# Small TensorE products of a hybrid encoder layer padded to the whole array, or their parts stacked in the rows of one float32r product

## Chip, core and metric

The kernel runs on one core of one Trainium2 chip. The metric is the device time of one execution in microseconds (us), taken as the median of several runs. Engines are named TensorE (PE in rows, its weight loads PEld), VectorE (DVE), ScalarE (ACT), GpSimd (POOL) and SyncE (SP).

## What is computed

One layer of an encoder on 512 tokens of width 2048, ahead of which 16 learned meta tokens stand (L = 528). Three branches read column groups of one projection and are projected back together:

```python
h = concatenate([meta, x], axis=1)
u = rmsnorm(h, norm_w)
proj = u @ w_in
(gq, gk, gv, ggate, gcode, dq, dk, dv, dgate, z, xbc, dt_raw) = jnp.split(proj, split_idx, axis=-1)
glog = log_sigmoid(einsum('blzr,zrk->blzk', gcode, gla_wa2) + gla_ba) / GLA_TAU
o_gla = rmsnorm(bidirectional(gla_chunk_scan, ...), gla_norm_w) * silu(ggate)
o_diff = diff_attention(dq, dk, dv, lam, lambda_init, rel_bias, diff_norm_w) * silu(dgate)
y = bidirectional(ssd_chunk_scan, (xs, dt, a, Bm, Cm), ...)
o_ssd = rmsnorm((y + xs * ssd_D) * silu(z), ssd_norm_w)
h = h + concatenate([o_gla, o_diff, o_ssd], axis=-1) @ w_out
out = rmsnorm(h, final_norm_w)[:, N_META:]
```

Everything is float32. The meta tokens are the reason for most products with few rows: 528 positions are four blocks of 128 and one of 16.

## The kernel before, in words

The two large projections run in float32r, with each operand split into a high and a low part and three products summed (`uh`, `ul` for the normalised tokens, `whi`, `wlo` for the weights, `mm3` for the smaller products of this kind). Weights stream in as `wraw`; ScalarE rounds them to `whi` (L72) and VectorE subtracts to `wlo` (L132). All products go through the helper `mm` at L39, so their rows in the profile have one line and are told apart by tiles: results into `pm` buffers are the large projections, results into `pb` buffers the small products. Each pool has four buffers of PSUM.

The program is written as generators of tiles in plain order: load and normalise, transpose the tokens (`features`, L265), project the decay and B/C columns, SSD group 0 and 1 (`ssd_group`), then gated linear attention in head pairs (`decays`, `tok`), the relative-bias table, differential attention (`attention`, `softmax`, `values`), output projection, final norm. The order on each engine is not that of the text: a scheduler simulates the program and lays each engine's queue by it. Each engine then works its queue strictly in order, and waits on semaphores for operands and free buffers.

The products with few contraction rows, all in plain float32 (two instructions each in the profile; the transposes are one):

- L265, 16 meta-token rows of `mt` transposed against a 16 x 16 identity, 16 times, one for each 128 columns of width
- L322 and L324, the 64 rows of `comb` (decay and gate codes) transposed, five times
- L513 in `state`, `Btm` (16 rows x 128) by `xe` (16 x 512), the meta tokens' contribution to the SSD state, once in each of the two groups, after the loop over the four chunks of the group
- L585 in `decays`, `wa` (32 rows: the low-rank gate weights of both directions) by `comb`, two halves of 264 positions for each of four heads: eight products
- L651, `Em` (64 rows x 16) transposed, once for each head
- L671, `km` (16 rows x 64) by `vm`, once for each head
- L747, `rb` (32 buckets x 4 heads) by a one-hot matrix of 512, 512 and 16 columns, which makes the relative-bias table
- L830 in `values`, `wT2` by `vm`, both 16 rows, the meta tokens' share of attention's output, once for each of four heads and four query blocks

```python
v, vm = vd[h]
nc.tensor.transpose(po[0:NM, 128:256], w_[:, 512:528], ident)
wT2 = small.tile([NM, P], F32, name="wT2", bufs=2)
nc.vector.tensor_copy(wT2, po[0:NM, 128:256])
for c in range(4):
    mm(nc, po[:, 0:P], wT[:, c * P:(c + 1) * P], v[:, c], c == 0, False)
mm(nc, po[:, 0:P], wT2, vm, False, True)
```

The table goes through DRAM: written as `tabd`, copied four times to `tabr` (L754), and read as one tile `bt` for each head (L773), all on the DMA queue that GpSimd issues. `bt` has one buffer, so the tile of the next head is issued when the last addition of the head before has read it. The gate weights `wa` are loaded by that queue too, at the start of the kernel (L568 to L570).

Of the kernel before, what the change touches and what calls it, by code (L numbers as in the profile page):

```python
# [42 lines left out]
def encoder_kernel(ctx, tc, x, meta, rel_bias, final_norm_w, norm_w, w_in, w_out, gla_wa2, gla_ba,  # L43
# [46 lines left out]
    nc.scalar.activation(warm, warm, AF.Exp)  # L90
    for i in range(2):
# [167 lines left out]
    def features(parts, us):  # L259
        for k in range(KT):  # L260
            pt = pb()
            n = 0
            for t in parts:
                rows = NM if t == 4 else P
                nc.tensor.transpose(pt[:, n:n + rows], xt[t, k // 4][0:rows, (k % 4) * P:(k % 4 + 1) * P],  # L265
                                    ident[0:rows, 0:rows])
                n += rows
            cpy(uh[k][:, us], pt[:, 0:n], scale=nw[:, k:k + 1])
            stt(ul[k][:, us], pt[:, 0:n], nw[:, k:k + 1], uh[k][:, us].bitcast(F32), ALU.mult, ALU.subtract)
# [178 lines left out]
    def ssd_group(g, em):  # L448
# [17 lines left out]
        Btm = small.tile([NM, P], F32, name="Btm", bufs=2)  # L466
# [25 lines left out]
        for c in range(NC):  # L492
            py = pb()
            for i, m in enumerate(em):
                if c == 0:
                    tt(m, m, sc, ALU.mult)  # L496
                for hh in (slice(0, 64), slice(64, P)):
                    mm(nc, py[hh, i * 64:(i + 1) * 64], m[:, c, hh], xk[c][:, i * 64:(i + 1) * 64])
            ys = slot("o" if g else "ya", [P, 512], name="ya")
            yacc[g, c] = ys  # L500
            gtt(h3(ys), h3(xk[c]), hb(dfac[:, c, G8]), ALU.mult)
            tt(ys, py, ys, ALU.add)
# [32 lines left out]
        Sf = state(0, 4, None)  # L535
        Sb = state(1, 3, None)
# [11 lines left out]
    def tok(acc, tag, cuts, name):  # L548
# [11 lines left out]
        vm = small.tile([NM, P], F32, name=name + "m", bufs=4 if name == "vd" else 2)  # L560
        nc.vector.tensor_copy(vm, pt[0:NM, 0:P])
# [16 lines left out]
    def decays(h, reset):  # L578
# [36 lines left out]
        Em = small.tile([64, NM], F32, name="Em", tag="Em")  # L615
# [12 lines left out]
    def gla_pair(p, dd):  # L628
# [7 lines left out]
        for i in range(2):  # L636
# [25 lines left out]
        for i in range(2):  # L662
# [3 lines left out]
            v, vm = tok(t1([(C_GV + h * P, P, 0)]), "ya", (NM, 0), "gv")  # L666
# [99 lines left out]
    vd = [tok(t1([(C_DV + h * P, P, 0)]), "ya", (0, 512), "vd") for h in range(4)]  # L766
# [50 lines left out]
    def values(h, b, w_, rr):  # L817
# [8 lines left out]
        wT2 = small.tile([NM, P], F32, name="wT2", bufs=2)  # L826
        nc.vector.tensor_copy(wT2, po[0:NM, 128:256])
# [117 lines left out]
def _consts():  # L945
# [14 lines left out]
    onehot = (np.arange(32)[:, None] == bucket[None, :]).astype(np.float32)  # L960
    pick = np.zeros((P, 2, 16), np.float32)
# [25 lines left out]
```

## Time and profile before

| what | value |
|---|---|
| runs, median (lowest to highest, n) | 935.36 us (935.08 to 935.91, 3) |
| the profiled execution | 932.87 us |
| its span, first to last instruction | 931.1 us |
| mean granted TensorE clock | 0.991 |
| TensorE busy | 896.7 us (96%), 5750 products |
| VectorE, ScalarE, GpSimd busy | 552.0, 377.1, 177.5 us |
| TensorE's longest wait | 12.2 us for the vectors' load at the start |
| DMA | 88.06 MB, 96 GB/s of HBM over the span |

In the rows below, times are in microseconds unless marked ns. `16*128` ahead of the shapes of a product is its contraction rows times its output partitions, so `128*32` is a product over all rows with 32 outputs. `x2` is the number of instructions that a row stands for; a timeline row gives the start of the first and the time until the end of the last. Matmuls are pipelined, so one starts before the other ends: the distance of two starts is what a product costs in a full queue, and the busy time of one is longer. In square brackets stands the idle time ahead of an instruction and what ended it.

### The profile page before, as it was taken

What the parts mean: (1) busy time and instruction counts of PE and PEld (TensorE: products, weight loads), DVE (VectorE), ACT (ScalarE), POOL (GpSimd) and SP (SyncE); (2) the same over time, 40 slices, a digit from 0 to 9 for tenths busy, and PEclk for the clock granted to TensorE, in tenths of its full rate; (3) what the DMA queues carried; (4) which work ended last, traced back from release to release, by engine and by line L of the source; (5) the groups of instructions that cost most, each with busy time, mean ns of one, the idle gap of its engine ahead of it and who ended that gap; (6) DMA issues with size and microseconds to landing.
All of it is one profiled execution on the core that took longest, in us unless ns stands there. A gap on an engine that the chain in (4) does not pass through costs nothing.

```text
span 931.1 us, 14454 instructions
## 1 busy us (share of the span) xinstructions
PE 896.7 (96%) x5750; PEld 787.2 (85%) x5750; DVE 552.0 (59%) x1043; ACT 377.1 (40%) x734; POOL 177.5 (19%) x212
## 2 busy tenths in 40 slices
PE   4998999999999999999999999999999999999996
PEld 3898998997778788999999999888888888888884
DVE  6569976989957686853642466665552633232334
ACT  6555524336434386734222345554332432121322
POOL 1006203449334412010040000000120001020200
PEclk9999999999999999999999999999999999999998
DMA  8322232321133234123236332324223442223224
GB/s 243 97 69 62 75 83 56 85 74 46 47 90 87 74 92 110 48 67 91 75 75 190 90 83 72 94 80 134 80 80 90 151 144 91 92 95 107 91 91 181
DMA packets 99523, 88.06 MB, mean 95 GB/s; under 512 B 8223, under 2 KB 75415, under 8 KB 99455
## 3 DMA queue, kind: packets, MB, share of 16 engines
q1 hardware_dynamic: 95183, 77.06, 29.2%
q0 software_dynamic: 1392, 4.84, 1.8%
q10 hardware_dynamic: 2880, 5.24, 1.7%
q8 instruction: 45, 0.74, 0.3%
q14 instruction: 23, 0.19, 0.1%
HBM read 82.91 MB, written 6.34 MB: 96 GB/s over the span
## 4 chain that ended last, share of the span: by engine, by line
PE 84%; DVE 8%; issue 2%; DMA 2%; ACT 2%; SPq 1%; POOL 0%; ACTq 0%; POOLq 0%; DVEq 0%
PE pm L39 71%; PE pb L39 9%; DVE acc L394 2%; DMA xt<-in_x_dram 1%; DVE wlo L132 1%; PE pb L867 1%; PE pb L821 1%; PE pb L265 1%; DMA gn<-in_diff_norm_w_dram 1%; SPq L86 1%; DVE sg L431 1%; SPq L214 0%; DVE m L496 0%; ACT whi L72 0%; DVE acc L392 0%
## 5 line engine op out<-in xcount | busy, mean ns | idle before, releaser
L132 DVE TENSOR_TENSOR wlo<-wraw,whi 128x1024 fp32r<-128x1024 f32 (+1 forms) x128 | 167.3, 1307 | 205.0 <-ACT whi L72 204.5
L72 ACT ACTIVATE whi<-wraw 128x1024 fp32r<-128x1024 f32 (+1 forms) x134 | 137.2, 1025 | 301.5 <-PE pm L39 228.6
L39 PE MATMUL pm<-ul,whi 128*128 128x272 f32 (+2 forms) x960 | 226.7, 301 | 0.0
L39 PE MATMUL pm<-uh,whi 128*128 128x272 f32 (+2 forms) x960 | 222.5, 299 | 0.0
L39 PE MATMUL pm<-uh,wlo 128*128 128x272 f32 (+2 forms) x928 | 217.1, 299 | 0.1
L39 PEld LDWEIGHTS pm<-ul,whi 128*128 128x128 f32 x960 | 156.7, 190 | 7.9 <-issue 3.0
L39 PEld LDWEIGHTS pm<-uh,whi 128*128 128x128 f32 x960 | 156.2, 191 | 5.8 <-ACT uh L72 0.3
L39 PEld LDWEIGHTS pm<-uh,wlo 128*128 128x128 f32 x928 | 150.7, 190 | 6.0 <-issue 0.7
L39 PE MATMUL pm<-wlo,uh 128*128 128x512 f32 x256 | 102.3, 400 | 0.2 <-DVE wlo L132 0.2
L39 PE MATMUL pm<-whi,ul 128*128 128x512 f32 x256 | 101.2, 396 | 0.0
L39 PE MATMUL pm<-wlo,mh 128*128 128x512 f32 x256 | 100.7, 395 | 0.0
L39 PE MATMUL pm<-whi,ml 128*128 128x512 f32 x256 | 100.4, 394 | 0.0
L39 PE MATMUL pm<-whi,uh 128*128 128x512 f32 x256 | 95.5, 398 | 0.0
L39 PE MATMUL pm<-whi,mh 128*128 128x512 f32 x256 | 90.3, 394 | 0.0
L115 POOL TENSOR_TENSOR rs_r<-rs_v,mhalf 128x1 f32<-128x1 f32 (+1 forms) x28 | 20.0, 715 | 275.8 <-DVE rs_v L114 203.8
L39 PEld LDWEIGHTS pm<-whi,ul 128*128 128x128 f32 x256 | 48.4, 189 | 11.5 <-issue 1.1
L39 PEld LDWEIGHTS pm<-wlo,uh 128*128 128x128 f32 x256 | 48.4, 189 | 11.4 <-DVE wlo L132 0.7
L39 PEld LDWEIGHTS pm<-whi,ml 128*128 128x128 f32 x256 | 48.2, 188 | 11.3
L39 PEld LDWEIGHTS pm<-whi,mh 128*128 128x128 f32 x256 | 48.1, 188 | 11.1
L39 PEld LDWEIGHTS pm<-whi,uh 128*128 128x128 f32 x256 | 48.3, 189 | 10.8
L39 PEld LDWEIGHTS pm<-wlo,mh 128*128 128x128 f32 x256 | 48.1, 188 | 10.9
L901 POOL TENSOR_TENSOR hx<-hx,fw 128x512 f32<-128x512 f32 x12 | 18.1, 1542 | 164.9 <-ACT junk L888 164.9
(291 smaller groups left out, 1186.3 us busy)
## 6 DMA issues: line engine op xcount, KB each, us to landing
wraw<-in_w_in_dram SPq DMA_DIRECT2D x96, 512.0 KB, 3.7
wraw<-in_w_out_dram SPq DMA_DIRECT2D x30, 512.0 KB, 3.6
xt<-in_x_dram SPq DMA_DIRECT2D x16, 256.0 KB, 5.7
hx<-in_x_dram ACTq DMA_DIRECT2D x16, 256.0 KB, 3.7
out_dram<-hx SPq DMA_DIRECT2D x16, 256.0 KB, 2.9
tabr<-tabd POOLq DMA_DIRECT2D x4, 520.0 KB, 9.0
bt<-tabr POOLq DMA_DIRECT2D x4, 456.0 KB, 3.7
fw<-in_final_norm_w_dram ACTq DMA_DIRECT2D x4, 256.0 KB, 4.5
```

The source lines that it names most:

```text
L39: nc.tensor.matmul(out, lhsT=lhsT, rhs=rhs, start=start, stop=stop)
L72: nc.scalar.activation(out, in_, AF.Copy, **kw)
L86: nc.sync.dma_start(xt[t, j], xv[t][:, j * 512:(j + 1) * 512])
L115: gtt(r[0:rows, 0:cols], v[0:rows, 0:cols], mhalf[0:rows, 0:cols], ALU.pow)
L132: tt(lo, raw, hi.bitcast(F32), ALU.subtract)
L265: nc.tensor.transpose(pt[:, n:n + rows], xt[t, k // 4][0:rows, (k % 4) * P:(k % 4 + 1) * P], ident[0:rows, 0:rows])
L394: stt(acc, xp[:, k:k + L], cw[:, k:k + 1], acc, ALU.mult, ALU.add)
L431: stt(sg[:, c], px[:, c * P:(c + 1) * P], Xs[:, 1, c, h:h + 1], sg[:, c], ALU.subtract, ALU.min)
L821: nc.tensor.transpose(pt[:, c * P:(c + 1) * P], w_[:, c * P:(c + 1) * P], ident)
L867: nc.tensor.transpose(pt[:, c * P:(c + 1) * P], src[:, j * P:(j + 1) * P], ident)
L901: gtt(hx[t, b], hx[t, b], fw[b], ALU.mult)
```

## The change

A tile `zp` of zeros (128 x 15 x 64) is cut into slots that hold the 16-row operands `vm` (four slots `vz`), `wT2` (two, `wz`), `km` (two, `kz`) and the 64-row `Em` (four, `ez`). Copies write only the filled rows, and the products run over all 128 rows. The meta-token tile `mt` and the lower half of `comb` are cleared by GpSimd, and their transposes use the whole identity. Three products get their high and low parts stacked in the contraction rows of one float32r product of 96 rows: `BE` and `XE` for the SSD meta tokens (high, high, low by high, low, high at rows 0, 32 and 64), `WA` and `CS` for the gates, `RB` and a one-hot matrix of 96 rows for the bias table. The meta tokens' SSD state `Sf = state(0, 4, None)` is written ahead of the chunk loop, which moves the definitions of `state` and `yoff` up, unchanged apart from the branch for `c == 4`. `wa` is no longer a constant of its own but takes a slot of the shared work pool. The scratch for software-issued DMA is set to 8192.

```diff
+    zp = const.tile([P, 15, 64], F32, name="zp")
+    nc.vector.memset(zp, 0.0)
+    vz = [zp[:, 2 * i:2 * i + 2].rearrange("p a b -> p (a b)") for i in range(4)]
...
+    XE = const.tile([96, 512], F32R, name="XE")
+    BE = const.tile([96, P], F32R, name="BE")
+    RB = const.tile([96, 4], F32R, name="RB")
+    cpy(XE, zp[0:96, 0:8].rearrange("p a b -> p (a b)"))
...
         mt = wpool.tile([P, 1024], F32, name="mt", tag="whi" if i else "wlo")
+        nc.gpsimd.memset(mt, 0.0)
...
-                nc.tensor.transpose(pt[:, n:n + rows], xt[t, k // 4][0:rows, (k % 4) * P:(k % 4 + 1) * P],
-                                    ident[0:rows, 0:rows])
+                nc.tensor.transpose(pt[:, n:n + P], xt[t, k // 4][:, (k % 4) * P:(k % 4 + 1) * P], ident)
...
     comb = const.tile([P, L], F32, name="comb")
+    nc.gpsimd.memset(comb[64:P], 0.0)
...
+    CS = const.tile([96, L], F32R, name="CS")
+    cpy(CS[0:32], comb[0:32])
+    cpy(CS[64:96], comb[0:32])
+    tt(CS[32:64], comb[0:32], CS[0:32].bitcast(F32), ALU.subtract)
...
-        nc.vector.tensor_copy(Btm, pt[0:NM, 0:P])
+        cpy(BE[0:NM], pt[0:NM, 0:P])
+        cpy(BE[32:32 + NM], pt[0:NM, 0:P])
+        tt(BE[64:64 + NM], pt[0:NM, 0:P], BE[0:NM].bitcast(F32), ALU.subtract)
...
             if c == 4:
-                mm(nc, p_, Btm, xe[0:rows])
+                cpy(XE[0:NM], xe[0:NM])
+                cpy(XE[64:64 + NM], xe[0:NM])
+                tt(XE[32:32 + NM], xe[0:NM], XE[0:NM].bitcast(F32), ALU.subtract)
+                mm(nc, p_, BE, XE)
...
-    wa = const.tile([32, 4, P], F32, name="wa")
+    WA = const.tile([96, 4, P], F32R, name="WA")
+    wa = slot("w", [32, 4, P], name="wa")
     nc.gpsimd.memset(wa, 0.0)
...
+    cpy(WA[0:32], wa)
+    cpy(WA[32:64], wa)
+    tt(WA[64:96], wa, WA[0:32].bitcast(F32), ALU.subtract)
...
-            mm(nc, pg[:, 0:HL], wa[:, h, :], comb[0:32, hs])
+            mm(nc, pg[:, 0:HL], WA[:, h, :], CS[:, hs])
...
-            nc.tensor.transpose(pt[0:NM, 0:64], Em, ident[0:64, 0:64])
-            km = small.tile([NM, 64], F32, name="km", bufs=2)
-            nc.vector.tensor_copy(km, pt[0:NM, 0:64])
+            nc.tensor.transpose(pt[0:NM, 0:P], ez[2 * p + i], ident)
+            km = kz[i]
+            nc.vector.tensor_copy(km[0:NM], pt[0:NM, 0:64])
...
+        ohr = slot("w", [96, 512], F32R, name="ohr")
+        cpy(ohr[:, 0:n], oh[:, 0:n])
-        mm(nc, p_[0:4, 0:n], rb, oh[:, 0:n])
+        mm(nc, p_[0:4, 0:n], RB, ohr[:, 0:n])
...
-        wT2 = small.tile([NM, P], F32, name="wT2", bufs=2)
-        nc.vector.tensor_copy(wT2, po[0:NM, 128:256])
+        wT2 = wz[b % 2]
+        nc.vector.tensor_copy(wT2[0:NM], po[0:NM, 128:256])
...
-    nc = bacc.Bacc("TRN2", target_bir_lowering=False, num_devices=1)
+    nc = bacc.Bacc("TRN2", target_bir_lowering=False, num_devices=1, dynamic_dma_scratch_size=8192)
```

Two places show how the scheduler lays the queues now. The first is TensorE at the SSD meta-token product of group 0, before:

```order
L39 MATMUL pm<-uh_120,wlo 128x272
L39 MATMUL pm<-uh_120,wlo 128x256
L39 MATMUL pm<-uh_121,whi 128x272
L39 MATMUL pm<-uh_121,whi 128x256
L487 MATMUL pb<-masks,acc 128x128 x4
L39 MATMUL pb<-xk,m 64x64 x64
L39 MATMUL pb<-xe,Btm 128x512
L39 MATMUL pm<-ul_137,whi 128x272
```

and in the changed kernel:

```order
L39 MATMUL pm<-uh_121,whi 128x272
L39 MATMUL pm<-uh_121,whi 128x256
L39 MATMUL pm<-ul_137,whi 128x272
L39 MATMUL pm<-ul_137,whi 128x256
L39 MATMUL pb<-XE,BE 128x512
L39 MATMUL pb<-xk,m 64x64 x64
L39 MATMUL pb<-xs,Bt 128x512 x3
L39 MATMUL pm<-uh_121,wlo 128x272
```

The product has moved from behind the 64 small products of the chunk loop (`xk,m`) to ahead of them, and the first product of the next state (`xs,Bt`) now stands right behind the 64, where before a column of the large projection stood.

The second is TensorE at the first gate products, before:

```order
L39 MATMUL pm<-whi,uh_122 128x512
L39 MATMUL pb<-Ss,CTs 128x512
L39 MATMUL pb<-comb,wa 128x264
L39 MATMUL pb<-Ss,CTs 128x512 x2
L39 MATMUL pb<-comb,wa 128x264 x2
L39 MATMUL pm<-wlo,uh_122 128x512
L39 MATMUL pm<-whi,ul_138 128x512
```

and in the changed kernel, where `CS,WA` are the stacked operands:

```order
L39 MATMUL pm<-wlo,uh_134 128x512
L39 MATMUL pm<-whi,ul_150 128x512
L39 MATMUL pm<-whi,uh_135 128x512
L39 MATMUL pm<-wlo,uh_135 128x512
L39 MATMUL pm<-whi,ul_151 128x512
L39 MATMUL pb<-CS,WA 128x264 x4
L39 MATMUL pm<-wlo,uh_134 128x512
L39 MATMUL pm<-whi,ul_150 128x512
```

Before, one and then two products stand between the last SSD output products (`Ss,CTs`); now four stand together, later, among the products of the next projection. What they wait for has moved too, on GpSimd, which issues the load of the gate weights. Before, at the start:

```order
L108 MEMSET mhalf 128x8
L241 MEMSET ssq 128x1 x5
L568 MEMSET wa 32x512
L608 MEMSET zr 64x4
L740 DMA rb<-in_rel_bias_dram 32x4
L882 MEMSET hss 128x4
L570 DMA wa<-in_gla_wa_dram 16x4x64 x2
```

and in the changed kernel, behind the SSD additions (`ya` is the running SSD output, `Sn` a state):

```order
L517 TENSOR_TENSOR xe<-xk,xef 128x512
L543 TENSOR_TENSOR ya<-ya,yo 128x512
L532 TENSOR_TENSOR Sn<-Sn,dec 128x512
L543 TENSOR_TENSOR ya<-ya,yo 128x512
L592 MEMSET wa 32x512
L649 MEMSET reset 128x528
L594 DMA wa<-in_gla_wa_dram 16x4x64 x2
L543 TENSOR_TENSOR ya<-ya,yo 128x512
```

The load stands one addition ahead of the end of the SSD part.

## Rows read from the trace of the kernel before

**Rows 1.** The chain that ended last, by line: share of the span.

```profile
PE pm L39 71%; PE pb L39 9%; DVE acc L394 2%; DMA xt<-in_x_dram 1%; DVE wlo L132 1%; PE pb L867 1%; PE pb L821 1%; PE pb L265 1%; DMA gn<-in_diff_norm_w_dram 1%; SPq L86 1%; DVE sg L431 1%; SPq L214 0%; DVE m L496 0%; ACT whi L72 0%; DVE acc L392 0%
```

**Rows 2.** Busy time by stretch: length, then PE, PEld, DVE, ACT, POOL.

```profile
165.00:260.00 95.00, 89.88 (x661) 79.33 (x660) 90.04 (x129) 42.13 (x86) 55.44 (x44) 0.98 0.23 62
260.00:700.00 440.00, 439.65 (x2923) 389.63 (x2922) 258.53 (x590) 189.15 (x381) 65.47 (x89) 1.00 0.32 89
```

**Rows 3.** TensorE's groups by shape: busy us, mean ns, idle before and its releaser.

```profile
L265 PE MATMUL pb<-masks,mt 16*128 16x16 f32 x16 | 3.9, 261 | 2.8 <-DVE ss L250 2.0 <-DVE ul L269 0.8
L39 PE MATMUL pb<-vdm,wT 16*128 16x128 f32 x32 | 7.7, 321 | 0.0
L39 PE MATMUL pb<-xe,Btm 16*128 16x512 f32 x4 | 2.2, 640 | 2.7 <-DVE ya L502 2.7
```

**Rows 4.** Timeline of TensorE in attention: start us, busy us, line, out<-in.

```profile
647.05 0.40 PE L39 MATMUL pm<-wlo,uh 128*128 128x512 f32 x1
647.28 1.05 PE L39 MATMUL pb<-vd,wT 128*128 128x128 f32 x8
648.27 0.48 PE L39 MATMUL pb<-vdm,wT 16*128 16x128 f32 x2
648.68 0.39 PE L39 MATMUL pb<-kh,qs 128*128 128x264 f32 x1
648.91 0.29 PE L39 MATMUL pb<-kl,qs 128*128 128x264 f32 x1
649.03 0.27 PE L821 MATMUL pb<-masks,p 128*128 128x128 f32 x1
```

**Rows 5.** Timeline of TensorE, products with a 32-column output.

```profile
71.38 1.94 PE L39 MATMUL pb<-mstr,at 128*32 128x128 f32 x16
73.24 0.51 PE L39 MATMUL pm<-uh,whi 128*128 128x272 f32 x2
73.59 0.29 PE L39 MATMUL pm<-ul,whi 128*128 128x272 f32 x1
```

**Rows 6.** Timeline of the weight loads of the same place in attention.

```profile
648.27 0.29 PEld L39 LDWEIGHTS pb<-vdm,wT 16*128 16x128 f32 x2
...
648.79 0.19 PEld L39 LDWEIGHTS pb<-kl,qs 128*128 128x128 f32 x1
```

**Rows 7.** Timeline of TensorE around one gate product.

```profile
370.95 0.28 PE L39 MATMUL pm<-uh,wlo 128*128 128x272 f32 x1
371.17 0.71 PE L39 MATMUL pb<-comb,wa 32*128 32x264 f32 x2
371.81 0.39 PE L39 MATMUL pm<-uh,wlo 128*128 128x256 f32 x1
372.03 0.29 PE L39 MATMUL pm<-uh,whi 128*128 128x272 f32 x1
```

**Rows 8.** Timeline of TensorE at the relative-bias table.

```profile
466.25 1.02 PE L39 MATMUL pb<-oh,rb 32*4 32x512 f32 x2
467.20 0.40 PE L39 MATMUL pm<-ul,whi 128*128 128x272 f32 x1
```

**Rows 9.** Timeline of TensorE at the first SSD meta-token product.

```profile
153.75 1.12 PE L39 MATMUL pb<-xe,Btm 16*128 16x512 f32 x2 [1.51 <-DVE ya L502]
154.80 0.39 PE L39 MATMUL pm<-ul,whi 128*128 128x272 f32 x1
```

**Rows 10.** Timeline of GpSimd, at the start and near 327 us.

```profile
0.94 0.52 POOL L568 MEMSET wa<- 32x512 f32 x1
2.33 1.06 POOL L570 DMA_DIRECT2D wa<-in_gla_wa_dram  x2
...
327.25 1.28 POOL L533 TENSOR_TENSOR ya<-ya,yo 128x512 f32<-128x512 f32 x1 [4.81 <-DVE yo L532]
```

**Rows 11.** The bias tile bt: who waited for it, and its landings.

```profile
  DVE p L804: 1.0, 2
DMA to landing us min/median/max: 3.3/3.7/8.5
```

More of the change, by code (lines that the diff above doesn't have):

```diff
@@ L90, in encoder_kernel @@
     nc.scalar.activation(warm, warm, AF.Exp)
+    zp = const.tile([P, 15, 64], F32, name="zp")
+    nc.vector.memset(zp, 0.0)
+    vz = [zp[:, 2 * i:2 * i + 2].rearrange("p a b -> p (a b)") for i in range(4)]
+    wz = [zp[:, 8 + 2 * i:10 + 2 * i].rearrange("p a b -> p (a b)") for i in range(2)]
+    kz = [zp[:, 12 + i] for i in range(2)]
+    ez = [zp[:, 14, NM * i:NM * i + NM] for i in range(4)]
+    XE = const.tile([96, 512], F32R, name="XE")
+    BE = const.tile([96, P], F32R, name="BE")
+    RB = const.tile([96, 4], F32R, name="RB")
+    cpy(XE, zp[0:96, 0:8].rearrange("p a b -> p (a b)"))
+    cpy(BE, vz[0][0:96])
+    cpy(RB, vz[0][0:96, 0:4])
     for i in range(2):
         mt = wpool.tile([P, 1024], F32, name="mt", tag="whi" if i else "wlo")
+        nc.gpsimd.memset(mt, 0.0)
         nc.sync.dma_start(mt[0:NM], meta[:, i * 1024:(i + 1) * 1024])
@@ L263, in features @@
             for t in parts:
-                rows = NM if t == 4 else P
-                nc.tensor.transpose(pt[:, n:n + rows], xt[t, k // 4][0:rows, (k % 4) * P:(k % 4 + 1) * P],
-                                    ident[0:rows, 0:rows])
-                n += rows
+                nc.tensor.transpose(pt[:, n:n + P], xt[t, k // 4][:, (k % 4) * P:(k % 4 + 1) * P], ident)
+                n += NM if t == 4 else P
             cpy(uh[k][:, us], pt[:, 0:n], scale=nw[:, k:k + 1])
@@ L321, in encoder_kernel @@
     for c in range(NC):
-        nc.tensor.transpose(ptd[:, c * P:c * P + 64], comb[0:64, NM + c * P:NM + (c + 1) * P], ident[0:64, 0:64])
+        nc.tensor.transpose(ptd[:, c * P:(c + 1) * P], comb[:, NM + c * P:NM + (c + 1) * P], ident)
     ptm = pb()
-    nc.tensor.transpose(ptm[0:NM, 0:64], comb[0:64, 0:NM], ident[0:64, 0:64])
+    nc.tensor.transpose(ptm[0:NM, 0:P], comb[:, 0:NM], ident)
+    CS = const.tile([96, L], F32R, name="CS")
+    cpy(CS[0:32], comb[0:32])
+    cpy(CS[64:96], comb[0:32])
+    tt(CS[32:64], comb[0:32], CS[0:32].bitcast(F32), ALU.subtract)
     dts = slot("w", [P, 3, 5, 32], name="dts")
@@ L489, in ssd_group @@
             cpy(xk[c][0:rows], pt[0:rows])
[L492 to L502, printed above, removed]
         def state(z, c, S0):
@@ L535, in ssd_group @@
         Sf = state(0, 4, None)
+        for c in range(NC):
+            py = pb()
+            for i, m in enumerate(em):
+                if c == 0:
+                    tt(m, m, sc, ALU.mult)
+                for hh in (slice(0, 64), slice(64, P)):
+                    mm(nc, py[hh, i * 64:(i + 1) * 64], m[:, c, hh], xk[c][:, i * 64:(i + 1) * 64])
+            ys = slot("o" if g else "ya", [P, 512], name="ya")
+            yacc[g, c] = ys
+            gtt(h3(ys), h3(xk[c]), hb(dfac[:, c, G8]), ALU.mult)
+            tt(ys, py, ys, ALU.add)
         Sb = state(1, 3, None)
@@ L546, in encoder_kernel, with tok @@
         ssd_group(g, ssd_decay(g))
-    def tok(acc, tag, cuts, name):
+    def tok(acc, tag, cuts, name, vm):
         vf = slot("ev", [P, L], name="vf")
@@ L559, in tok @@
         nc.tensor.transpose(pt[0:NM, 0:P], vf[:, rest:rest + NM], ident)
-        vm = small.tile([NM, P], F32, name=name + "m", bufs=4 if name == "vd" else 2)
-        nc.vector.tensor_copy(vm, pt[0:NM, 0:P])
+        nc.vector.tensor_copy(vm[0:NM], pt[0:NM, 0:P])
         return v, vm
-    wa = const.tile([32, 4, P], F32, name="wa")
+    WA = const.tile([96, 4, P], F32R, name="WA")
+    wa = slot("w", [32, 4, P], name="wa")
     nc.gpsimd.memset(wa, 0.0)
@@ L614, in decays @@
         nc.scalar.activation(E[2], E[2], AF.Exp, scale=1.0 / 16)
-        Em = small.tile([64, NM], F32, name="Em", tag="Em")
+        Em = ez[h][0:64]
         tt(Em, X[F, NM - 1:NM].broadcast_to([64, NM]), X[F, 0:NM], ALU.subtract)
@@ L734, in encoder_kernel @@
     gla_pair(1, gla_pair(0, dd))
-    rb = const.tile([32, 4], F32, name="rb")
+    rb = small.tile([32, 4], F32, name="rb")
     nc.gpsimd.dma_start(rb, rel_bias)
+    cpy(RB[0:32], rb)
+    tt(RB[32:64], rb, RB[0:32].bitcast(F32), ALU.subtract)
     tabd = dram.tile([4, NTAB], F32, name="tabd")
@@ L743, in encoder_kernel @@
         n = min(512, NTAB - i)
-        oh = slot("w", [32, 512], name="oh")
+        oh = slot("w", [96, 512], name="oh")
         nc.gpsimd.dma_start(oh[:, 0:n], onehot[:, i:i + n])
+        ohr = slot("w", [96, 512], F32R, name="ohr")
+        cpy(ohr[:, 0:n], oh[:, 0:n])
         p_ = pb()
-        mm(nc, p_[0:4, 0:n], rb, oh[:, 0:n])
+        mm(nc, p_[0:4, 0:n], RB, ohr[:, 0:n])
         tb = slot("w", [4, 512], name="tb")
@@ L764, in encoder_kernel @@
     nlam = ls[:, 2:3]
-    vd = [tok(t1([(C_DV + h * P, P, 0)]), "ya", (0, 512), "vd") for h in range(4)]
+    vd = [tok(t1([(C_DV + h * P, P, 0)]), "ya", (0, 512), "vd", vz[h]) for h in range(4)]
     od = [slot("ya", [P, 512], name="od") for _ in range(NC)]
@@ L960, in _consts @@
     onehot = (np.arange(32)[:, None] == bucket[None, :]).astype(np.float32)
+    onehot = np.concatenate([onehot, onehot, 0 * onehot])
     pick = np.zeros((P, 2, 16), np.float32)
```

3 lines of the change are left out of this document (1 added, 2 removed).

## Prediction

> **What bounds the kernel now.** First the chain of work that ended last: its two largest parts are TensorE's one matmul helper, 71% of the span into the pm buffers and 9% into the pb buffers [rows 1]. Then the busy times by stretch, to see where TensorE is the limit and where it only looks like it [rows 2]. From 260 to 700 us it is busy 439.65 of 440 us: there a microsecond taken from TensorE is a microsecond of the kernel. From 165 to 260 us VectorE is busy 90.04 of 95 us: there TensorE's time is partly covered by VectorE's. So a saving counts fully after 260 us and only in part before it.
>
> Third, the groups of TensorE's instructions by shape [rows 3]. A product in plain float32 stands there as two instructions, one in float32r as one. The 16-row product of attention (vdm,wT) has 32 instructions, the 16-row SSD product (xe,Btm) four, with 2.7 us idle ahead of two of them, and the meta-token transposes number 16. Their busy times, 7.7, 2.2 and 3.9 us, are the wrong price, since matmuls overlap. What counts is the step from start to start.
>
> Fourth, the starts around one 16-row product [rows 4]. A 512-column product takes a step of 0.23 us (647.05 to 647.28), a 264-column one 0.12 (648.91 to 649.03). A float32 instruction of 128 columns takes 0.11: sixteen from 71.38 to 73.24 are 1.86 us with 0.10 at their end [rows 5]. Eight such, the two 16-row ones and one 264-column one should take 10 x 0.11 + 0.12 = 1.22 us. They take 648.91 - 647.28 = 1.63. The missing 0.41 us lies at the borders: 0.11 ahead of the 16-row pair, 0.19 in it and behind it, 0.11 at the next product. The weight loads tell why [rows 6]: the full-array load of 648.79 runs 0.11 us after the matmul of 648.68 began and 0.12 ahead of its own at 648.91, beside the running one; the 16-row load starts at 648.27, with its own matmul, and so does the first full one behind it, at 648.68. Where few rows follow the whole array or the other way round, load and matmul stand one behind the other.
>
> **The change part by part.**
>
> Attention, 16 sites. vm and wT2 get zero rows up to 128, so the product fits its neighbours. It keeps its two instructions of 128 columns (0.22 us) and loses the border: 16 x 0.41 = 6.6 us, all in the stretch where TensorE is full. The zero rows are written once, at the start; per site VectorE writes the same 16 rows as before, so nothing is added.
>
> Gate product, eight. Three parts of 32 rows are stacked into one 96-row float32r instruction. Before, from 370.95 to 372.03 us [rows 7], a 272-column product, one gate product and a 256-column one took 1.08 us. After it is 3 x 0.12 = 0.36: 0.72 less. Four stand alone like this one. Four come as two pairs, where the second of a pair has no border but still two float32 instructions: 0.64 between the starts (371.17 to 371.81), less the 0.10 of a border, is 0.54, against 0.12: 0.42. So 4 x 0.72 + 2 x (0.72 + 0.42) = 5.2 us. No row shows a 96-row product. I take it for a whole-array one, since those that show a border fill half of the rows or less. If it is not, the border of 0.3 stays at each place: between 3.4 and 5.2. The four Em transposes, 64 rows before, lose a border of about 0.2 each (0.10 in, 0.10 out): 0.8 us.
>
> Relative-bias table, two products of 512 columns and one of 16. Before, 0.95 us from a product to what follows it [rows 8]. After, one float32r instruction, but its output has four columns. A 32-column output of 128 rows shows a border too: 73.24 to 73.59 is 0.35 for two products that take 0.25 elsewhere [rows 5], and 0.10 on leaving. So I leave it the border: 0.95 - 0.23 - 0.10 = 0.62, twice, 1.2 us (1.9 if a narrow output cost nothing). For the same reason I take nothing for gvm,km, whose four products have 64 output columns: 0, between a loss of 0.3 and a gain of 1.3 (four borders of 0.3).
>
> SSD meta-token product, two. 1.05 us from its start to the next [rows 9] and a border of 0.10 after, now 0.23: 0.92 each, 1.8 us. It also moves ahead of the 64 small products of its group, so that the 1.51 us wait for VectorE's ya [rows 9] and its like in the second group (2.7 in all [rows 3]) no longer stand in front of it. VectorE is nearly full there [rows 2], so part of that wait returns at the next product that needs it, the xs product, which now stands right behind the 64. I take 1.2 of 2.7, between 0 and 2.7. In exchange VectorE makes one more 16 x 512 part (about 0.67 us by a 128 x 512 of the same kind) in each group: minus 0.7 for the group in which VectorE is full.
>
> Transposes at the start. Each meta-token site loses about 0.2 us. Eleven of the 16 lie ahead of the 2.0 us stop at the ss reduction [rows 3], which waits for a load on VectorE, so they gain nothing; five gain 1.0. Against it the clearing of mt now stands ahead of its load on GpSimd: two of 128 x 1024, some 1 us each by the 0.52 of the 32 x 512 memset [rows 10]. The same stop hides it. Without that cover it is up to 2 us. The comb transposes lose two borders, 0.4 us.
>
> New wait. The gate weights are loaded not at the start but when a slot is free: behind a GpSimd addition that ends before 322.5 (the next begins at 327.25 after 4.81 idle [rows 10]). Memset 0.5, another memset of that size 0.5, two issues 1.1 [rows 10], 3.7 to landing as the bias tiles on the same queue have it [rows 11], two copies and a subtraction on ACT and VectorE about 1.7: near 330. In the new order TensorE comes to the first gate product at some 331 on this clock. It just fits; behind it in TensorE's queue stands the whole rest of the projection, so a late load is a bare wait. I charge 0.8, between 0 and 3.
>
> Sum: 6.6 + 5.2 + 0.8 + 1.2 + 1.8 + 1.2 + 1.0 + 0.4 - 0.7 - 0.8 = 16.7. I round to 16.5, since the early half must pass the VectorE-bound stretch. The profiled execution took 932.87 us, giving 916.4; the median of the runs is 935.36, 2.5 above it, and by that the forecast is **918.9 us**.
>
> One rule speaks against all of this. The Trainium skill ("TensorE: Matmul & The Clock Gate", Part 3, what overlaps and what doesn't) says that a weight load overlaps matmuls in flight only when its row group differs. By it a padded product, in the same rows as its neighbours, would be serial like all others, and only the fewer instructions would save time, about 5 us. The trace disagrees: the load of 648.79 overlaps in the same rows [rows 6].
>
> **The rivals.**
>
> *Few rows are not what costs, or 96 rows still count as few.* Then the gate and SSD products keep borders of 0.3 us at eight places (2.4), and where a third of attention's 0.41 has another cause than the rows, 2.1 more stay: 16.5 - 4.5 = 12, 923.4 us. For it: no row shows 96 rows. Against it: in the timeline of the 16-row product nothing but the row count changes at the borders [rows 4].
>
> *The early gains are swallowed.* What lies before 260 us (1.8 + 1.2 + 1.0 + 0.4) is covered by VectorE or by the waits that move. Left are 6.6 + 5.2 + 0.8 + 1.2 - 0.8 = 13, 922.4 us. For it: VectorE at 95% of 165 to 260.
>
> *All waits go.* The whole 2.7 idle, the narrow outputs' borders (0.7 + 1.3) and no late gate load: 16.7 + 1.5 + 2.0 + 0.8 = 21, 914.4 us.
>
> *Padding saves nothing and only the instruction counts do.* The borders would come from changes of shape that remain. Gate 8 x 0.42 = 3.4, table 1.2, SSD 0.6: 5.2, 930.2 us. That is also what the rule cited above gives.
>
> *Slower: the bias loads of attention.* The change sets the scratch of the software-issued DMA queue to 8192. The four bias tiles go through that queue, and VectorE already waits for them twice, 1.0 us [rows 11]. If their landings grow, the last three grow on the path, since each is issued when the head before frees its buffer and TensorE's next scores wait behind VectorE. From 16.5 / 3 = 5.5 us more per landing the kernel is slower; at 10 us more each it is 30 - 16.5 = 13.5 slower, 949 us. Against it: that queue carries few loads at a time.
>
> **How the numbers follow.** The forecast 0.58; 96 rows or the row count wrong 0.13; early gains swallowed 0.14; all waits gone 0.07; padding saves nothing 0.04; slower 0.04. The range leaves out the last two and the far edge of the third: 913.5 to 926.5 us; the unknown bounds (narrow outputs 2.0, 96 rows 1.8, idle 1.5, gate load 2.2) lie inside it. About 0.2%, 1.9 us, is what a measurement of this kernel can tell from no change. Faster 0.93, same 0.03, slower 0.04.
>
> **What would show it.** In the profile after: the pair vdm,wT steps at 0.11 with no border, and its weight loads start before the matmul ahead of them ends; the gate product one instruction at a step of 0.12; the table's product still with a border; no idle of ya ahead of the SSD product; TensorE busy about 880 us. The forecast is wrong if the 96-row product shows borders, if a wait on WA stands ahead of the first gate product, if the xs product takes over the idle of ya, or if VectorE's waits for the bias tiles grow beyond 5 us.

## The result, and the profile after

The changed kernel takes 918.55 us (median of 4 runs, 917.57 to 921.69), beside 935.46 us for the kernel before (4 runs, 935.08 to 935.91): a ratio of 0.9825, 95% interval 0.98 to 0.9849. The forecast was 918.9. The profiled execution took 917.57 us, its span is 915.8.

The chain that ended last, by line, answers to [rows 1]: the matmul helper's share into `pm` has gone from 71% to 65%, and VectorE's `wlo` (L146) from 1% to 2%.

```profile
PE pm L39 65%; PE pb L39 7%; DVE acc L413 2%; DVE wlo L146 2%; DMA xt<-in_x_dram 2%; PE pb L898 1%; PE pb L852 1%; DVE sg L450 1%; ACT whi L72 1%; DVE acc L411 1%; DVE xs L459 1%; DMA gn<-in_diff_norm_w_dram 1%; SPq L228 1%; DVE m L552 1%; DVE m L453 0%
```

TensorE is busy 876.9 us, 19.8 less than before. By stretch, with the columns of [rows 2], TensorE is still the limit after 260 us, though no longer without gaps: it idles 3.1 us between 260 and 700, where it idled 0.35.

```profile
165.00:260.00 95.00, 89.18 (x647) 78.73 (x646) 90.63 (x128) 43.05 (x89) 58.89 (x45) 0.98 0.26 73
260.00:700.00 440.00, 436.90 (x2961) 394.11 (x2960) 259.15 (x592) 193.08 (x387) 65.50 (x91) 1.00 0.33 91
```

The attention site, in the timeline of TensorE, answers to [rows 4]; the padded operands are now called `zp`.

```profile
634.33 1.06 PE L39 MATMUL pb<-vd,wT 128*128 128x128 f32 x8
635.22 0.39 PE L39 MATMUL pb<-zp 128*128 128x128 f32 x2
...
635.57 0.28 PE L39 MATMUL pb<-kl,qs 128*128 128x264 f32 x1
```

From the first `vd,wT` to the second score product it is 635.57 - 634.33 = 1.24 us, where it was 1.63: 0.39 less, with the same number of instructions. The weight loads, which answer to [rows 6], now begin while the matmul ahead still runs:

```profile
635.11 0.30 PEld L39 LDWEIGHTS pb<-zp 128*128 128x128 f32 x2
635.34 0.19 PEld L39 LDWEIGHTS pb<-kh,qs 128*128 128x128 f32 x1
```

The load for the padded product starts at 635.11, 0.11 us ahead of its matmul, as a neighbour's does.

A gate product [rows 7] and the table's product [rows 8], timeline of TensorE:

```profile
365.24 0.29 PE L39 MATMUL pm<-ul,whi 128*128 128x272 f32 x1
365.36 0.29 PE L39 MATMUL pb<-CS,WA 96*128 96x264 f32 x1
365.49 0.28 PE L39 MATMUL pm<-ul,whi 128*128 128x256 f32 x1
365.61 0.41 PE L39 MATMUL pm<-uh,wlo 128*128 128x272 f32 x2
...
459.53 0.40 PE L39 MATMUL pm<-uh,whi 128*128 128x272 f32 x2
459.77 0.40 PE L39 MATMUL pb<-ohr,RB 96*4 96x512 f32 x1
460.01 0.38 PE L39 MATMUL pb<-Sp,E 128*128 128x128 f32 x2
```

The gate product takes a step of 0.13 us (365.36 to 365.49), and the three products that took 1.08 us [rows 7] take 0.37 (365.24 to 365.61). The table's product takes 0.24 (459.77 to 460.01), a plain 512-column step, with no border on either side, although it has four output columns. That was not foreseen.

The idle times of TensorE, as the timeline shows them in brackets, have changed places. The ones that matter:

```profile
30.85 0.33 PE L279 MATMUL pb<-masks,mt 128*128 128x128 f32 x1 [2.36 <-DVE ul L282]
...
230.80 0.50 PE L39 MATMUL pm<-wlo,uh 128*128 128x512 f32 x1 [2.33 <-DVE wlo L146]
...
258.11 0.50 PE L39 MATMUL pb<-xs,Bt 128*128 128x512 f32 x1 [1.55 <-ACT xs L72]
...
342.32 0.51 PE L39 MATMUL pm<-uh,wlo 128*128 128x512 f32 x1 [0.53 <-DVE rs_v L128]
...
348.84 0.50 PE L39 MATMUL pm<-uh,wlo 128*128 128x512 f32 x1 [0.66 <-DVE wlo L146]
...
386.05 0.46 PE L39 MATMUL pb<-gv,A 128*128 128x128 f32 x2 [1.58 <-DVE A L724]
```

The waits for `ya` ahead of the SSD product [rows 9] are gone. In their place stand 1.55 us for `xs` at 258 and 2.33 for `wlo` at 231 (the kernel before waits for `wlo` there too, 0.22 us in its first profile and 1.77 in that of the scratch run below), and where the gates were relieved, 0.53, 0.66 and 1.58 us at 342, 349 and 386.

### The profile page after: what moved, and what is told of

The parts are those of the page before. It is cut to its first block, busy times and chain, and to the rows that moved or that the text cites. A ratio compares the mean times of both kernels' runs of the same rounds, so it can differ in the third digit from the quotient of the medians.

```text
span 915.8 us, 14461 instructions
## 1 busy us (share of the span) xinstructions
PE 876.9 (96%) x5737; PEld 779.9 (85%) x5737; DVE 554.0 (60%) x1049; ACT 383.7 (42%) x753; POOL 183.7 (20%) x215
## 4 chain that ended last, share of the span: by engine, by line
PE 75%; DVE 12%; ACT 4%; issue 4%; DMA 2%; SPq 1%; POOL 1%; ACTq 0%; POOLq 0%; DVEq 0%
PE pm L39 65%; PE pb L39 7%; DVE acc L413 2%; DVE wlo L146 2%; DMA xt<-in_x_dram 2%; PE pb L898 1%; PE pb L852 1%; DVE sg L450 1%; ACT whi L72 1%; DVE acc L411 1%; DVE xs L459 1%; DMA gn<-in_diff_norm_w_dram 1%; SPq L228 1%; DVE m L552 1%; DVE m L453 0%
## 5 line engine op out<-in xcount | busy, mean ns | idle before, releaser
L146 DVE TENSOR_TENSOR wlo<-wraw,whi 128x1024 fp32r<-128x1024 f32 (+1 forms) x128 | 163.7, 1280 | 212.6 <-ACT whi L72 212.3
L39 PE MATMUL pm<-ul,whi 128*128 128x272 f32 (+2 forms) x960 | 224.4, 300 | 0.0
L39 PE MATMUL pm<-uh,wlo 128*128 128x256 f32 (+2 forms) x928 | 214.6, 297 | 1.2 <-DVE wlo L146 0.7
```

The source lines that it names most:

```text
L39: nc.tensor.matmul(out, lhsT=lhsT, rhs=rhs, start=start, stop=stop)
L146: tt(lo, raw, hi.bitcast(F32), ALU.subtract)
```

## The experiments

Profiles of one program differ by 1.5 to 2 us where TensorE's granted clock falls to the lower level for a few microseconds, so stages are compared in the traces beside the total times.

**How many rows make a product "few"?** One kernel, 16 row counts:

```diff
-        mm(nc, po[:, 0:P], wT2, vm, False, True)
+        R = (16, 32, 48, 64, 65, 72, 80, 96, 97, 112, 120, 124, 127, 128, 96, 64)[4 * h + b]
+        mm(nc, po[:, 0:P], wT2[0:R], vm[0:R], False, True)
```

> The changed kernel, with attention's 16 meta-token products contracting 16, 32, 48, 64, 65, 72, 80, 96, 97, 112, 120, 124, 127, 128, 96 and 64 rows (the operands are zero beyond row 16, so the result is the same). Theory (a border is paid where a product's rows fall in a smaller row tile than its neighbours'): from the first vd,wT to the second score product the 64-row and smaller sites take 1.6 us as before the change, those of 65 rows and more 1.24 us as after it; nothing in between. Rival (only a product of all 128 rows is free): 65 to 127 rows also take 1.6. Rival (the time grows with the unused rows): a slope from 1.6 to 1.24. Total: within 2 us of the changed kernel.

The 64-row site and, below the dots, the 65-row site, in the timeline of TensorE:

```profile
573.34 1.05 PE L39 MATMUL pb<-vd,wT 128*128 128x128 f32 x8
574.32 0.48 PE L39 MATMUL pb<-zp 64*128 64x128 f32 x2
...
574.97 0.28 PE L39 MATMUL pb<-kl,qs 128*128 128x264 f32 x1
...
585.45 1.05 PE L39 MATMUL pb<-vd,wT 128*128 128x128 f32 x8
586.34 0.39 PE L39 MATMUL pb<-zp 65*128 65x128 f32 x2
...
586.69 0.28 PE L39 MATMUL pb<-kl,qs 128*128 128x264 f32 x1
```

With 64 rows the site takes 574.97 - 573.34 = 1.63 us, with 65 it takes 586.69 - 585.45 = 1.24. The 16, 32 and 48-row sites are like the first, those of 72 to 128 like the second. It is a step between 64 and 65, not a slope. Padding to 128 is more than is needed, and 96 stacked rows are as good as 128. The run, a single one, took 922.21 us, 3.7 more than the changed kernel and not within the 2 expected. In attention it loses 1.9 us, its five sites with a border; 2.7 it is behind already at the first `kh,qs` (530.03 against 527.36), in instructions that are the same in both.

**How many output columns?** The same for the width of the output, which leaves out the meta tokens' share of attention's output:

```diff
-            mm(nc, po[:, 0:P], wT[:, c * P:(c + 1) * P], v[:, c], c == 0, False)
-        mm(nc, po[:, 0:P], wT2, vm, False, True)
+            mm(nc, po[:, 0:P], wT[:, c * P:(c + 1) * P], v[:, c], c == 0, c == 3)
+        M = (4, 16, 24, 31, 32, 33, 48, 64, 65, 80, 96, 112, 127, 128, 32, 64)[4 * h + b]
+        mm(nc, po[0:M, 256:384], wT2[:, 0:M], vm)
```

> The changed kernel, with attention's 16 meta-token products at 128 rows but 4, 16, 24, 31, 32, 33, 48, 64, 65, 80, 96, 112, 127, 128, 32 and 64 output columns, written to an unused stretch of the buffer; the meta tokens' share of attention's output is left out. The trace after shows no border at 4 output columns and one at 64. Theory (a border belongs to outputs of 32 to 64 columns, that is where a column tile is chosen): 1.5 us or more at 32, 33, 48 and 64, and 1.24 at the others, 31 and fewer included. Rival (only the exact sizes 32 and 64 are tiles): 33 and 48 are free too. Rival (every width up to 64 pays, the table's product was hidden): 4 to 31 also take 1.5. Total within 2 us of the changed kernel.

64 columns and, below the dots, 65:

```profile
605.79 1.05 PE L39 MATMUL pb<-vd,wT 128*128 128x128 f32 x8
606.77 0.43 PE L39 MATMUL pb<-zp 128*64 128x128 f32 x2
...
607.36 0.29 PE L39 MATMUL pb<-kl,qs 128*128 128x264 f32 x1
...
613.60 1.05 PE L39 MATMUL pb<-vd,wT 128*128 128x128 f32 x8
614.49 0.38 PE L39 MATMUL pb<-zp 128*65 128x128 f32 x2
...
614.84 0.28 PE L39 MATMUL pb<-kl,qs 128*128 128x264 f32 x1
```

At 64 columns 607.36 - 605.79 = 1.57 us, at 65 columns 614.84 - 613.60 = 1.24. Every width from 4 to 64 shows the border, so the theory fell and the last rival held, for plain float32. The run took 921.6 us, 3.1 more than the changed kernel where 2 had been expected; its ten narrow sites at some 0.3 each make as much. But then why does the table's product with four columns show none? It is float32r. So the same site was given one float32r product, with rows and columns varied:

```diff
...
+        R = (16, 32, 64, 65, 80, 96, 96, 96, 96, 96, 96, 96, 96, 96, 96, 96)[4 * h + b]
+        M = (128, 128, 128, 128, 128, 128, 4, 16, 31, 32, 48, 64, 65, 96, 127, 128)[4 * h + b]
+        mm(nc, po[0:M, 256:384], BE[0:R, 0:M], XE[0:R, 0:128])
```

> The changed kernel with attention's 16 meta-token products replaced by one-instruction float32r products of the SSD operands BE and XE, 128 moving columns, written to an unused stretch of the buffer (the meta tokens' share of attention's output is left out): 16, 32, 64, 65, 80 and 96 rows with 128 output columns, then 96 rows with 4, 16, 31, 32, 48, 64, 65, 96, 127 and 128 output columns. Theory (in float32r only the rows decide): a border of about 0.3 us at 16, 32 and 64 rows, none at any width, as the table's 4-column product showed none. Rival (narrow outputs pay in float32r as they do in float32): a border at 4 to 64 columns too, and the table's product was an exception.

64 rows with 128 columns and, below the dots, 96 rows with 64 columns:

```profile
560.73 1.06 PE L39 MATMUL pb<-vd,wT 128*128 128x128 f32 x8
561.72 0.32 PE L39 MATMUL pb<-XE,BE 64*128 64x128 f32 x1
...
562.20 0.29 PE L39 MATMUL pb<-kl,qs 128*128 128x264 f32 x1
...
646.97 1.05 PE L39 MATMUL pb<-vd,wT 128*128 128x128 f32 x8
647.78 0.30 PE L39 MATMUL pb<-XE,BE 96*64 96x128 f32 x1
...
648.10 0.29 PE L39 MATMUL pb<-kl,qs 128*128 128x264 f32 x1
```

With 64 rows the site takes 562.20 - 560.73 = 1.47 us, with 64 columns 648.10 - 646.97 = 1.13. All ten widths read like the second, 16 and 32 rows like the first. So few rows cost in both forms, few columns only in plain float32. (The run took 916.89 us, with 16 instructions fewer.)

**What is the attention part worth?** Back to 16 rows, with every queue in the order of the changed kernel:

```diff
-        mm(nc, po[:, 0:P], wT2, vm, False, True)
+        mm(nc, po[:, 0:P], wT2[0:NM], vm[0:NM], False, True)
```

> The changed kernel with attention's 16 meta-token products cut back to 16 rows; the order of every queue is that of the changed kernel. Theory (the border of few rows costs 0.39 us a site, all on the path): 16 x 0.39 = 6.2 us slower than the changed kernel, 924.8. Rival (the gain came from the order or from fewer slow spells of the clock): within 1 us of the changed kernel, 918.6.

It took 926.14 us (925.31 to 928.38), ratio to the kernel before 0.9929 (0.9909 to 0.9949). Ahead of attention its trace is 1.89 us behind that of the changed kernel (first `kh,qs` at 529.25 against 527.36), and behind attention 8.15 (`masks,od` at 746.27 against 738.12): 6.26 us in attention alone, 16 x 0.39. The 1.89 us ahead of it are in instructions that are the same in both and are not the rows' doing: this trace has a granted clock of 0.83 and 0.86 in 30 to 40 and 80 to 90 us, where the changed kernel has 1.00. The ratios of different comparisons are not to be set side by side either: the executions of the kernel before had a median granted clock of 0.992 in this one, and of 0.989 in that of the control below.

**What is the gates' gain made of?** First 64 of the 96 stacked rows, then padding without stacking:

```diff
-            mm(nc, pg[:, 0:HL], WA[:, h, :], CS[:, hs])
+            mm(nc, pg[:, 0:HL], WA[0:64, h, :], CS[0:64, hs])
```

> The changed kernel with the eight gate products contracting 64 of their 96 stacked rows, still one float32r instruction each; the product of the gate codes' high part with the weights' low part is left out. Theory (border by rows): a border of about 0.3 us comes back at each of the four places where gate products stand (four together, two, one, one): 1.2 us slower than the changed kernel, 919.8. Rival (the gain at the gates is the instruction count alone): no border in the timeline, no difference.

```diff
-    WA = const.tile([96, 4, P], F32R, name="WA")
-    wa = slot("w", [32, 4, P], name="wa")
+    wa = const.tile([P, 4, P], F32, name="wa")
...
-            mm(nc, pg[:, 0:HL], WA[:, h, :], CS[:, hs])
+            mm(nc, pg[:, 0:HL], wa[:, h, :], comb[:, hs])
```

> The changed kernel with the gate products over 128 padded rows in plain float32 (the weights and comb zero below row 32), nothing stacked, the weights loaded at the start. Theory (rows cost the border, float32 costs the second instruction): no border in the timeline, but two instructions a product of 264 columns, 0.48 to 0.54 us a product against 0.12: 8 x 0.4 = 3.2 us of TensorE more, of which 1 to 3 show, since the wait for A near 386 us takes some back. Rival (stacking does nothing, padding all): within 0.5 us.

With 64 rows the border is back: the group of four takes 0.67 us from its start to the next product, where it took 0.49 (325.36 to 325.85), and the products on both sides come 0.1 later. But the total is 920.53 us (ratio 0.9867, 0.9846 to 0.9888), and the two traces drift apart by only 0.4 us between 300 and 450 us: the rest disappears in the waits of that stage. With padding alone the stretch of [rows 7] is 0.68 us (370.56 to 371.24), beside 1.08 before and 0.37 after, so of its 0.71 us padding brings 0.40 and stacking 0.31. That kernel took 923.36 us (ratio 0.9878, 0.9853 to 0.9902); between 310 and 440 us its trace falls about 3 us further behind that of the changed kernel. But there it has a fall of the granted clock (third number from the end) that the changed kernel has not:

```profile
330.00:340.00 10.00, 8.12 (x40) 7.05 (x39) 9.77 (x21) 8.64 (x19) 0.00 (x0) 0.83 0.23 63
```

A mean of 0.83 over 10 us costs 10 x 0.17 = 1.7 us. So of the expected 3.2 about 1.5 shows, within the theory's 1 to 3. The weights are loaded at the start here and the gate products stand earlier in TensorE's queue, so this is not the stacking alone.

**The move of the SSD state, and a control.** The changed kernel again:

> The changed kernel once more, unchanged, as the control for the runs beside it. Theory (the early part of the first profile was ahead by 1.9 us because a spell of half clock was missing in it, not because of the change): 918 to 922 us; a profile whose granted clock is 0.991 to 0.993 lies 1.9 us behind the first one by 118 us, and keeps that distance. Rival (the early gain is the change's own): the profile repeats the first one's times to 0.3 us.

and with the state behind the chunk loop:

```diff
-        Sf = state(0, 4, None)
         for c in range(NC):
...
+        Sf = state(0, 4, None)
         Sb = state(1, 3, None)
```

> The changed kernel with the SSD meta-token state written behind the chunk loop again, where it stood before the change; its product stays the stacked one. Theory (the move takes the wait for ya from the path, and about half of it returns at the xs product): 1.2 us slower than the changed kernel, 0 to 2.7, with idle for ya ahead of XE,BE again. Rival (the move only shifts the wait, since VectorE is full there): within 0.5 us. Rival (the move made the new waits for wlo near 231 us and xs near 258 us, 3.9 together): 1 to 3 us faster.

The control took 919.8 us (918.11 to 921.19), ratio 0.9828 (0.9806 to 0.9849); without the move 919.82, ratio 0.9831 (0.9814 to 0.9847). In the total the move is worth nothing. With the state behind the loop `ya` is waited for again, longer than in the kernel before, and the waits for `xs` and `wlo` are shorter in exchange. TensorE's waits in that kernel (us in total, times, longest):

```profile
PE pb L39 <- DVE ya L555: 4.9, 2, 3.1
...
PE pm L39 <- DVE wlo L146: 1.8, 1, 1.8
...
PE pb L39 <- DVE xs L459: 0.9, 1, 0.9
```

The move does change where the time goes. These are two of the five places at which the scratch run below is measured (there 274.32 and 457.11), in the kernel without the move:

```profile
274.87 1.06 ACT L72 ACTIVATE whi<-wraw 128x1024 fp32r<-128x1024 f32 x1 [2.61 <-PE pm L39]
...
452.54 0.71 PE L39 MATMUL pb<-gv,ko 128*128 128x128 f32 x4
```

At 274 it is 0.55 us behind the kernel before, at 457 it is 4.57 ahead: start and SSD bring nothing, the gate stage 5.1. Each of these two traces has two falls of the clock before 274 us and none in between.

The control's profile shows how two executions of one program part. By stretch, granted clock third from the end, first the control and then the first profile of the same kernel:

```profile
80.00:90.00 10.00, 10.00 (x64) 9.63 (x63) 8.64 (x17) 7.80 (x24) 6.19 (x5) 0.83 0.21 54
```

```profile
80.00:90.00 10.00, 10.00 (x77) 9.70 (x77) 9.83 (x22) 8.16 (x25) 6.62 (x5) 1.00 0.30 76
```

A mean of 0.83 over 10 us is a stay at the lower of the two levels (1.2 instead of 2.4 GHz) that costs 1.7 us. TensorE had been idle for 2.86 us ahead of 80 us in both executions, and the clock fell in one. At 121 us the control is 2.0 behind, as its theory had it. It does not keep that distance: a second fall between 255 and 265 us, again 0.83 against 1.00, makes it 3.6 at 452.

**Three attempts at more.** The wide `km`, whose product then has 128 output columns:

```diff
-    kz = [zp[:, 12 + i] for i in range(2)]
+    kz = [zp[:, 12 + 2 * i:14 + 2 * i].rearrange("p a b -> p (a b)") for i in range(2)]
...
-            mm(nc, pt[0:64, 0:P], km, vm)
+            mm(nc, pt[:, 0:P], km, vm)
```

> The changed kernel with km widened by 64 zero columns, so that its four products have 128 output columns; all queues keep their order. Theory (an output of 64 columns or fewer pays a border of 0.3 us in a float32 product): 4 x 0.3 = 1.2 us faster where TensorE is full, less what the wait for A near 386 us takes back, so 0.6 to 1.2 faster. Rival (all of it is taken back by VectorE's waits in this stage): no difference.

918.16 us (916.57 to 918.86), ratio 0.9814 (0.9797 to 0.983) beside the control's 0.9828: the intervals overlap, but the traces show it: 1.1 us are gained between 390 and 470 us and kept to the end. It has the lowest median here. On top of it, the low part of `XE` on GpSimd:

```diff
-                tt(XE[32:32 + NM], xe[0:NM], XE[0:NM].bitcast(F32), ALU.subtract)
+                gtt(XE[32:32 + NM], xe[0:NM], XE[0:NM].bitcast(F32), ALU.subtract)
```

> The changed kernel with km widened to 128 columns and the subtraction for the low part of XE put on GpSimd, since VectorE is full where the second SSD group runs. Theory (VectorE sets the end there): the wait for xs near 258 us or that for wlo near 231 shrinks, 0.7 to 1.4 us less than with the wide km alone, 1.8 to 2.5 less than the changed kernel. Rival (the longer chain through GpSimd delays the stacked SSD product by as much): no better than the wide km alone, 1.1 less than the changed kernel.

It made things worse: 923.31 us, ratio 0.9902 (0.9864 to 0.994), with 4.97 us of waiting for `xs` at 263 us. (Its trace passes `gv,ko` 4.35 us after that of the wide `km`, 456.80 against 452.45; about 1.8 of this is clock, a longer stay at the lower level behind that wait.) And, again on top of the wide `km`, the gate weights loaded and stacked at the start:

```diff
+    WA = const.tile([96, 4, P], F32R, name="WA")
+    wa = slot("w", [32, 4, P], name="wa")
...
     dts = slot("w", [P, 3, 5, 32], name="dts")
```

> The changed kernel with km widened to 128 columns and the gate weights loaded and stacked at the start, right after CS; the first gate products then stand between the last SSD output products again, as before the change. Theory (the late load put the gate products late, so that VectorE's decay work is late and TensorE waits for it at 344 and 350 us, 1.2 together, and for A near 388 us, 1.7): these waits go, up to 2.9 us faster than with the wide km alone (ratio 0.9814 to the kernel before), 0.978 to 0.980. Rival (VectorE makes A as fast as it can, and TensorE, relieved of its borders, just comes to it sooner): the wait for A stays at 1.5 us or more, and the ratio stays within 0.0007 of 0.9814.

It took 919.19 us (915.79 to 921.91), ratio 0.9837 (0.9814 to 0.986): nothing gained. The waits near 344 and 350 us are gone, but others have come: 0.96 us for `th` at 333, 0.88 for `XE` at 253, and at 36 us 1.95 for `whi`, where the kernel with the wide `km` waits 0.38 for `uh`. At `A` the timeline of TensorE shows:

```profile
387.91 0.46 PE L39 MATMUL pb<-gv,A 128*128 128x128 f32 x2 [1.71 <-DVE A L724]
```

The wait for `A` stays at 1.71 us, so the late load was not its cause. There the rival held, but not in its ratio, which was to stay within 0.0007 of 0.9814: the waits that went were made good by new ones.

**The DMA scratch alone,** on the kernel before:

```diff
-    nc = bacc.Bacc("TRN2", target_bir_lowering=False, num_devices=1)
+    nc = bacc.Bacc("TRN2", target_bir_lowering=False, num_devices=1, dynamic_dma_scratch_size=8192)
```

> The kernel before with nothing changed but the scratch of the software-issued DMA queue set to 8192, as the change sets it; every queue keeps its order. Theory (that queue carries few loads at a time): no difference, 933 to 937 us, the bias tiles landing in 3.7 us as before. Rival (the slower case of the prediction): landings of the bias tiles several microseconds longer and VectorE's wait for them grown from 1.0 us, slower by three times that. Its profile is also a second look at the unchanged order: where spells of half clock fall, and how many, against the three of the first profile.

933.08 us, ratio 0.9999 (0.9979 to 1.002). The bias tiles land as before, in 3.6 us by the median, and VectorE's wait for them is 1.0 us. This trace is also a look at the order of the kernel before without a fall of the clock up to 150 us, so the stages can be measured against the first profile after, at five places that both pass (first the scratch kernel, then the changed one):

```profile
121.50 0.60 PE L462 MATMUL pb<-masks,acc 128*128 128x128 f32 x4
...
274.32 1.06 ACT L72 ACTIVATE whi<-wraw 128x1024 fp32r<-128x1024 f32 x1 [2.15 <-PE pm L39]
...
457.11 0.60 PE L39 MATMUL pb<-gv,ko 128*128 128x128 f32 x3
...
534.60 0.29 PE L39 MATMUL pb<-kh,qs 128*128 128x264 f32 x1
...
737.01 0.71 PE L867 MATMUL pb<-masks,ya 128*128 128x128 f32 x5
```

```profile
121.35 0.60 PE L481 MATMUL pb<-masks,acc 128*128 128x128 f32 x4
...
271.19 1.06 ACT L72 ACTIVATE whi<-wraw 128x1024 fp32r<-128x1024 f32 x1 [3.99 <-PE pm L39]
...
451.88 0.49 PE L39 MATMUL pb<-gv,ko 128*128 128x128 f32 x2
...
527.36 0.29 PE L39 MATMUL pb<-kh,qs 128*128 128x264 f32 x1
...
723.61 0.60 PE L898 MATMUL pb<-masks,ya 128*128 128x128 f32 x4
```

The wait for the bias tiles is 0.5 us in the changed kernel itself, with landings of 3.6. The lead of the changed kernel over the scratch kernel is 0.15 us at 121, 3.1 at 274, 5.2 at 457, 7.2 at 535 and 13.4 at 737, and stays there. Of the step at 274, 1.7 us are put down to a fall of the clock that only the scratch kernel has, near 150 us (0.83 between 150 and 160); both have one between 230 and 240. So by stage: the start 0.15, SSD 1.3, the gates and linear attention 2.1, the table 2.0, attention 6.2; 11.7 in all.

## Why the prediction was right, and where its working was not

The direction, the mechanism of the border and the total were right. That the total came out within 0.4 us is partly luck: the terms add up to 16.7 us and the stages to 11.7, and what fills most of the gap is the granted clock, which was not in the sum.

- *Attention, 16 x 0.41 = 6.6.* Right: 0.39 a site, 6.2 us on the path, and all of it shows, as TensorE is the limit there. Confirmed by putting the 16 rows back.
- *The 96-row product is a whole-array one.* Right, and more sharply than assumed: 65 rows are enough.
- *Table 1.2, because its narrow output keeps a border.* Wrong by 0.8: it gained 2.0. The step that failed carried a border seen in plain float32 [rows 5] over to float32r. The forecast's own upper bound, 1.9, was the case.
- *km 0, for its 64 output columns.* Right; widening it brings the 1.1 us that the prediction gave as the upper part of its bound (1.3).
- *Gates 5.2, Em 0.8, late load -0.8: 5.2 net.* The price of a product was right (0.72 predicted, 1.08 to 0.37 measured). What failed is "there a microsecond taken from TensorE is a microsecond of the kernel": TensorE now waits 1.58 us for `A` and 0.53 + 0.66 near 342 and 349 us, work that VectorE finishes later than TensorE comes to it. Between the places of 274 and 457 us it waits 0.2 us in the scratch kernel and 3.1 in the changed one, so 5.0 us were saved and 2.1 are left. The wait for the late gate weights, for which 0.8 was charged, did not come. Ahead of `A` it is VectorE that has no time left, as the stretch up to the end of `A` shows (third engine):

```profile
375.46:385.90 10.44, 8.88 (x108) 8.31 (x108) 10.16 (x26) 7.54 (x16) 0.20 (x1) 1.00 0.19 52
```

  The kernel without the move bears this out: it comes to the stage without the early lead, waits 0.9 us in it and gains 5.1. (Its queues are laid otherwise too, so the late arrival is not tried by itself.)
- *SSD 1.8 + 1.2 - 0.7 = 2.3.* 1.3 by 274 us, and not for the reasons given. Without the move the relieved product brings nothing there, since VectorE sets the pace [rows 2]; in these traces it is the move that brings the lead. But the lead is not kept: clear of the extra fall of the clock the changed kernel is 5.23 - 1.7 = 3.5 us ahead at 457, the one without the move 4.57. Early lead and gate saving run into the same limit, VectorE's work up to `A`. This is what the rival of swallowed early gains said; only they are swallowed behind 260 us, not ahead of it.
- *Start 1.0 and comb 0.4.* 0.15. Waits for `xt`, `ul` and `uh` took it back, the stop near 30 us among them (2.36 us now, 2.02 before).
- *Clock.* Not in the sum at all. The 11.7 us of the stages lie 3.7 below the 15.4 us between the medians in the control's comparison (935.16 and 919.8). Runs of one program show what the clock does: the ten of the scratch kernel go from 930.41 us at a mean granted clock of 0.995 to 937.4 at 0.987, 0.9 us for each 0.001 (a line through all ten gives 0.8). In the control's comparison the kernel before has a median clock of 0.989 and the changed kernel 0.992: 2.3 to 2.6 us by that slope, which leaves 1.1 to 1.4 us unexplained, within what the interval allows. Whether the change raised the clock or these runs happened to have it higher is open: in another comparison the kernel before had 0.992 as well. That fewer idle gaps make fewer falls of the clock fits the waits for `ya` that are gone, but no run here showed it.

The rivals: padding that saves nothing is refuted by the map of the rows. From 64 to 65 rows nothing changes but the row count, and the weight load moves from its matmul's own start (574.32 for both) to 0.11 us ahead of it (586.23 and 586.34). The Trainium skill ("TensorE: Matmul & The Clock Gate", Part 3, what overlaps and what doesn't) says that a weight load overlaps matmuls in flight only when its row group differs; the trace does not agree, as the load of 586.23 and those around it use the same rows. The slower case is refuted too: the smaller scratch changes neither landings nor time.

## What to carry to other kernels

A plain float32 or float32r product of 64 rows or fewer among whole-array products costs 0.3 to 0.4 us at its borders, measured at 128 and 264 columns; zero rows up to 65 or more, written once, take that away, and stacking the high and low parts in the rows takes the second instruction too. Price such an edit by start-to-start steps, and credit it fully only where the engine that feeds TensorE has slack: here attention gave all 6.2 us, the gate stage two of five, and all five where the kernel came to it later. Moving work past a wait brings a lead that the next stage can take back where another engine is full.

## What had not been expected

- The border is a step between 64 and 65, in rows and in columns: 1.63 against 1.24 us, and 1.57 against 1.24.
- Narrow outputs, from 4 to 64 columns, pay in plain float32 and not in float32r.
- The moved SSD product wins time by 274 us and loses more by 457, where TensorE waits 3.1 us instead of 0.9.
- Runs of one program differ by 7 us with the granted clock; the clock fell behind an idle of 2.86 us in one execution of a program and not in another.
